# Per-token factors by a transpose and a DRAM round trip, and a two-pass chunk, in a three-branch trunk layer

## The chip, the cores and the metric

The kernel runs on one core of one Trainium2 chip, in one launch. The metric is the device time of that core in microseconds (us). TensorE is written PE, VectorE DVE, ScalarE ACT, GpSimd POOL and SyncE, which issues nearly all DMAs here, SP.

## What is computed

One decoder layer over 2048 tokens of width 1024, with 16 meta tokens in front. The reference, cut to what matters:

```python
xn = rms_norm(h, norm_w)
proj = jnp.einsum('btd,dn->btn', xn, w_in)          # 12*512 + 8 + 3*1024 columns
q = rms_norm(heads(sb_q), sb_qn); k = rms_norm(heads(sb_k), sb_kn)
o_sb = stick_breaking_attention(q, k, v, valid) * silu(sb_z)
beta = sigmoid(gd_b) * vmask                        # gd_b, gd_a: 4 columns each
g = -exp(a_log) * softplus(gd_a + dt_bias)
o_gd = rms_norm(gated_delta_rule_chunked(l2_norm(gq), l2_norm(gk), gv, beta, g)) * silu(gd_z)
o_hg = rms_norm(hgrn2_chunked(silu(hg_q), hk, hg_i * vmask, log(forget))) * silu(hg_z)
y = sum(sigmoid(mix[b]) * (o_b @ w_branch[b]) for b in (sb, gd, hg))
out = h + y @ w_out
```

All of it is float32. The norms of x, of the attention's keys and of the gated branch's keys each give one factor per token.

## The kernel before

Activations lie transposed: 128 features on the partitions, tokens along the free axis. The sequence is worked in four passes (`j` = 0 to 3) of 512 tokens; pass 0 also carries the 16 meta tokens, in columns 0 to 15 of tiles 528 wide. A float32 product is made of three matmul passes on rounded parts (`mm3`, L146: high times high, high times low, low times high), so one **chunk** (128 output columns of the projection, `proj`, L206) is 8 x 3 = 24 matmul passes of 512 columns, in pass 0 twice 24 of 264 columns where the meta tokens are needed. `load_w` (L126) brings a chunk's weights in two halves. In pass 0 it loads raw weights (two buffers `wraw`), has ACT round them (L136) and POOL or DVE subtract (L110), and writes both parts back to DRAM (L140); in later passes it reads them back (L132). Either way they go into five half-chunk buffers, `w2`.

The dense work is one Python generator, `dense_work` (L1219). For each pass it projects four attention heads (key, query, value, gate: `sb_proj`, L305), the chunk of the eight columns `gd_b` and `gd_a` (`gdn_rows`, L501), the gated heads (key, query, value: `gdn_proj`, L599), and then branch products with their gates, the third branch's projections, and the output product. Each chunk ends with `yield END`. The loop at L1292 weaves the sequential parts (the attention `sb_scan`, `gdn_mats`, `gdn_scan`, `hg_scan`) into it: `adv(n)` runs the dense work alone for n chunk ends, `weave(scan, us, n)` lets a scan run beside n of them. A pass has 85 ends.

Small steps behind a chunk are put off: `later(fn)` runs `fn` after the next chunk's matmuls, `later2` after the one behind that. The framework's scheduler then fixes one order of instructions for each engine; every engine and the SP queue work theirs in that order. There are three PSUM banks `acc` for the dense work, and 18 buffers `D` of 128 x 528 in SBUF for most of its tiles.

The steps that the change touches:

- **A factor per token, for all features.** `sum_cols` (L259) transposes squares to tokens on partitions (L276) and adds them up, one column per 128 tokens; `rsqrt` (L112) takes the power on POOL (L117). To multiply a tile with features on the partitions, the factor is needed as a row repeated on every partition. `row_bcast` (L152) makes it on PE: each column, broadcast to 128 columns, is transposed against the identity, four times for the four token blocks (L156) and once more, 16 columns wide, for the meta tokens (L160). The result stays in a PSUM bank `acc`.
- **Its readers.** The norm of x copies it to a `D` tile (L250), which `norm_x` (L178) multiplies with. `sb_proj` does it after the query's sums: one `rsqrt` for key and query, then in `post_r` (L341), behind the gate chunk, the transposes, the multiplication L343, a rounding on ACT (L344) and a subtraction. `gdn_proj` does the same in its `post_r` (L624) with the multiplication L626.
- **The chunk of eight columns.** `gdn_rows` runs `proj` over 128 columns of which eight (0 to 3, 32 to 35) are not zero, copies 36 rows out of PSUM (L506) and transposes them in four blocks (L515), 36 wide.

Of the kernel before, what the change touches and what calls it, by code (L numbers as in the profile page):

```python
# [7 lines left out]
F32 = mybir.dt.float32  # L8
# [7 lines left out]
P = 128  # L16
D = 1024
# [22 lines left out]
def kernel(  # L40
# [45 lines left out]
    def p_acc():  # L86
        return ps_acc.tile([P, 512], F32, tag="acc", name=nm("acc"))
# [63 lines left out]

    def row_bcast(r, cols, mcol):  # L152

        pt = p_acc()
        for n, c in enumerate(cols):
            nc.tensor.transpose(pt[:, n * P : (n + 1) * P], r[:, c : c + 1].broadcast_to([P, P]), ident)  # L156
        res = [(slice(META, WQ), pt)]
        if mcol is not None:
            pm = p_acc()
            nc.tensor.transpose(  # L160
                pm[:, :META], r[:META, mcol : mcol + 1].broadcast_to([META, P]), ident[:META, :META]
            )
            res.append((slice(0, META), pm[:, :META]))
        return res

# [6 lines left out]
    def norm_x(j, xt, rb):  # L172

        c0 = 0 if j == 0 else META
        xh, xl = [], []
        for k in range(KC):
            t = xt[k]
            nc.vector.scalar_tensor_tensor(  # L178
                t[:, c0:], t[:, c0:], nw[:, k : k + 1], rb[:, c0:], ALU.mult, ALU.mult
            )  # L180
# [42 lines left out]
    def norm_stats(j):  # L223
# [15 lines left out]
        ncol = NT + (j == 0)  # L239
        rb = slot("D")  # L240

# [6 lines left out]
        def bcast(r):  # L248
            for sl, v in row_bcast(r, list(range(NT)), NT if j == 0 else None):
                nc.scalar.copy(rb[:, sl], v)  # L250

# [53 lines left out]
    def sb_proj(j, xs, h, st):  # L305
# [10 lines left out]
        v_ = cols_tile(j)  # L316
        later(lambda: sum_cols(sq, v_, 0, 8 if m0 else None))
        yield END
# [14 lines left out]
        def post_q():  # L333
            sum_cols(sq2, v_, 4)
            ncol = 8 + m0
            r = rsqrt(v_[:, :ncol], P, ncol)
            nc.vector.tensor_copy(rq[:, :NT], r[:, NT : 2 * NT])
            nc.vector.tensor_scalar(rq[:, NT:], r[:, NT : 2 * NT], -1.0, None, ALU.mult)
            later(lambda: post_r(r))

        def post_r(r):  # L341
            for sl, v in row_bcast(r, list(range(NT)), 8 if m0 else None):
                nc.vector.scalar_tensor_tensor(kraw[:, sl], kraw[:, sl], wk, v, ALU.mult, ALU.mult)  # L343
# [157 lines left out]
    def gdn_rows(j, xs, st):  # L501
# [3 lines left out]
        raw = slot("D")  # L505
        yield from proj(j, xs, CH_BA, True, lambda ps, a, b: nc.scalar.copy(raw[:36, a:b], ps[:36]))  # L506
        nt = NT + m0
# [4 lines left out]
        def post():  # L512
            pt = p_acc()
            for n in range(NT):
                nc.tensor.transpose(  # L515
                    pt[:, n * 36 : n * 36 + 36], raw[:36, META + n * P : META + (n + 1) * P], ident[:36, :36]
                )
            c8 = slot("c8", (P, 2, H, 5), F32, 1)
            if m0:
                nc.gpsimd.memset(c8, 0.0)  # L520
                pm = p_acc()
                nc.tensor.transpose(pm[:META, :36], raw[:36, :META], ident[:36, :36])
                for q in range(2):
                    nc.vector.tensor_copy(c8[:META, q, :, 4], pm[:META, 32 * q : 32 * q + H])
            ptv = pt[:, : NT * 36].rearrange("p (n c) -> p c n", n=NT)
            for q in range(2):
                nc.vector.tensor_copy(c8[:, q, :, :NT], ptv[:, 32 * q : 32 * q + H])
            nc.scalar.activation(bcol[:, :, :nt], c8[:, 0, :, :nt], AF.Sigmoid)
# [70 lines left out]
    def gdn_proj(j, xs, hs, st):  # L599
# [5 lines left out]
        def head(h):  # L605
# [11 lines left out]
            def post_q():  # L617
                sum_cols(sqq, v_, 4)
                ncol = 8 + m0
                r = rsqrt(v_[:, :ncol], P, ncol)  # L620
                nc.vector.tensor_scalar(aq, r[:, 4:8], SCALE, None, ALU.mult)
                later(lambda: post_r(r))

            def post_r(r):  # L624
                for sl, v in row_bcast(r, list(range(NT)), 8 if m0 else None):
                    nc.vector.tensor_mul(kk[:, sl], kk[:, sl], v)  # L626

# [664 lines left out]
    for j in range(nq):  # L1292
        adv(5)
        sb_us = 4 * (2.0 + 2.7 * j) + 0.8 * (5 + 4 * j)
# [98 lines left out]
```

## Time and profile before

| | |
|---|---|
| median of 3 runs | 2872.62 us (2872.39 to 2875.82) |
| the profiled execution: its time | 2878.11 us |
| the profiled execution: its span | 2876.0 us |
| PE busy | 2786.5 us, 97% |
| DVE, ACT, POOL busy | 1524.5, 932.1, 760.0 us |
| DMA | 522.74 MB, 182 GB/s on average |
| granted PE clock | 0.993 |

All shares are of the span. A row of the groups gives line, engine, operation, tiles (out<-in), shape and count, then the busy time in all and the mean duration in ns of one, and behind a second bar the engine's idle time just before, with what ended it. Matmuls overlap: a row of the timeline gives the start, so the distance of two starts is what one of them adds. A row of the waits reads: engine and line that waited, engine and line waited for, us in total, times, longest. For DMAs the last number is the time from issue to landing.

### The profile page before, as it was taken

The numbers are of one execution on the slowest core, as the hardware profiler recorded it, in microseconds if no ns is written. First come the engines' busy times: TensorE is split into PE (matmuls) and PEld (weight loads), VectorE is DVE, ScalarE is ACT, GpSimd is POOL, SyncE is SP. The second block draws the span as 40 slices with busy tenths as digits, with TensorE's granted clock in tenths as the row PEclk, the third lists the DMA queues.
The fourth block names the chain that finished last, engine by engine and source line by source line (L and its number), as shares of the span: only waits on it lengthen the run. The fifth ranks groups of instructions, "written<-read, shape, count | busy, mean of one in ns | idle before, by whom it ended". The sixth has DMA issues, their size and how long they took to land.

```text
span 2876.0 us, 42134 instructions
## 1 busy us (share of the span) xinstructions
PE 2786.5 (97%) x15691; PEld 2325.4 (81%) x15691; DVE 1524.5 (53%) x3069; ACT 932.1 (32%) x2123; POOL 760.0 (26%) x1012
## 2 busy tenths in 40 slices
PE   5999999998999999999999999999999999999999
PEld 4898788886788888888888888888888777787887
DVE  4467637635257543654156855555415677627521
ACT  4555233333245312113045531211314555121110
POOL 4556213333123401212022421111302233302111
PEclk9999999999999999999999999999999999999999
DMA  6667655667754664446754456344674443653546
GB/s 203 237 214 230 230 193 189 227 233 260 252 170 148 193 181 133 139 153 226 227 190 163 155 161 186 106 142 147 227 227 147 141 139 125 197 155 103 155 153 212
DMA packets 198288, 522.74 MB, mean 182 GB/s; under 512 B 40448, under 2 KB 41536, under 8 KB 198084
## 3 DMA queue, kind: packets, MB, share of 16 engines
q1 hardware_dynamic: 197796, 519.98, 55.6%
q8 instruction: 124, 2.03, 0.3%
q14 instruction: 80, 0.66, 0.1%
q10 hardware_dynamic: 288, 0.07, 0.0%
HBM read 399.13 MB, written 120.84 MB: 181 GB/s over the span
## 4 chain that ended last, share of the span: by engine, by line
PE 81%; DVE 7%; DMA 6%; ACT 2%; POOL 2%; issue 1%; SPq 1%; ACTq 0%; DVEq 0%; POOLq 0%
PE acc L147 21%; PE acc L149 21%; PE acc L148 20%; DMA wraw<-in_w_in_dram 2%; PE z L1011 2%; PE tr L445 2%; PE acc L276 1%; PE av L147 1%; PE av L148 1%; PE av L149 1%; PE z L147 1%; PE z L149 1%; PE z L148 1%; DVE D L178 1%; DMA wraw<-in_w_out_dram 1%
## 5 line engine op out<-in xcount | busy, mean ns | idle before, releaser
L147 PE MATMUL acc<-xh,w 128*128 128x512 f32 (+1 forms) x2568 | 989.8, 386 | 15.4 <-ACT w L136 4.1
L149 PE MATMUL acc<-xh,w 128*128 128x512 f32 (+1 forms) x2568 | 974.6, 380 | 0.4 <-POOL w L110 0.4
L148 PE MATMUL acc<-xl,w 128*128 128x512 f32 (+1 forms) x2568 | 966.6, 376 | 7.9 <-DVE xl L110 7.9
L147 PEld LDWEIGHTS acc<-xh,w 128*128 128x128 f32 x2568 | 486.9, 190 | 97.0 <-ACT w L136 4.2
L148 PEld LDWEIGHTS acc<-xl,w 128*128 128x128 f32 x2568 | 487.5, 190 | 88.1 <-DVE xl L110 8.4
L149 PEld LDWEIGHTS acc<-xh,w 128*128 128x128 f32 x2568 | 485.6, 189 | 85.6 <-POOL w L110 0.8
L110 POOL TENSOR_TENSOR w<-wraw,w 128x512 fp32r<-128x512 f32 x110 | 145.4, 1323 | 346.7 <-ACT w L136 327.9
L136 ACT CAST w<-wraw 128x512 fp32r<-128x512 f32 x186 | 115.0, 618 | 251.9 <-DMA wraw<-in_w_in_dram 104.8
L421 POOL TENSOR_TENSOR S<-S,S 128x256 f32<-128x256 f32 (+2 forms) x108 | 95.2, 882 | 382.9 <-DVE S L413 217.5
L413 DVE TENSOR_TENSOR_SCAN S<-S,cc,zero 128x272 f32<-128x272 f32 (+2 forms) x152 | 144.1, 948 | 82.2 <-ACT S L407 81.7
L147 PE MATMUL acc<-ob,w 128*128 128x512 f32 x384 | 156.4, 409 | 11.9 <-DVE D L1083 5.5
L407 ACT ACTIVATE S<-z,rq 128x128 f32<-128x128 f32 (+4 forms) x216 | 116.8, 541 | 129.1 <-PE z L149 95.2
L148 PE MATMUL acc<-ob,w 128*128 128x512 f32 x384 | 153.4, 400 | 0.0
L149 PE MATMUL acc<-ob,w 128*128 128x512 f32 x384 | 152.3, 397 | 0.0
L592 DVE SCALAR_TENSOR_TENSOR D<-D,cw,D 128x512 f32<-128x512 f32 (+1 forms) x144 | 125.2, 869 | 23.1 <-ACT D L590 20.7
L110 DVE TENSOR_TENSOR S<-tr,S 128x512 fp32r<-128x512 f32 (+4 forms) x176 | 105.1, 606 | 39.8 <-ACT S L449 39.1
L1085 POOL TENSOR_TENSOR y<-y,g 128x512 f32<-128x512 f32 x32 | 49.7, 1558 | 285.8 <-DVE g L1083 285.8
L1067 ACT ACTIVATE g<-acc 128x512 f32<-128x512 f32 x64 | 38.3, 598 | 261.9 <-PE acc L149 247.2
L116 POOL TENSOR_SCALAR nu<-nv 128x8 f32<-128x8 f32 (+4 forms) x40 | 15.3, 383 | 397.2 <-DVE nv L888 231.1
L408 ACT ACTIVATE S<-z,rq 128x128 f32<-128x128 f32 (+4 forms) x216 | 116.3, 538 | 0.0
L449 ACT CAST S<-tr 128x512 fp32r<-128x512 f32 (+4 forms) x176 | 91.0, 529 | 59.4 <-PE tr L445 58.1
L445 PE MATMUL tr<-ident,S 128*128 128x128 f32 (+1 forms) x608 | 100.9, 273 | 3.9 <-POOL S L421 3.2
(325 smaller groups left out, 4700.7 us busy)
## 6 DMA issues: line engine op xcount, KB each, us to landing
w<-wk SPq DMA_DIRECT2D x558, 512.0 KB, 3.5
wk<-w SPq DMA_DIRECT2D x186, 512.0 KB, 2.9
wraw<-in_w_in_dram SPq DMA_DIRECT2D x146, 256.0 KB, 3.8
D<-in_xq_dram SPq DMA_DIRECT2D x56, 256.0 KB, 4.7
S<-rows SPq DMA_DIRECT2D x48, 256.0 KB, 4.5
S<-dv SPq DMA_DIRECT2D x48, 256.0 KB, 4.5
out_dram<-D SPq DMA_DIRECT2D x32, 256.0 KB, 4.7
S<-dk SPq DMA_DIRECT2D x24, 264.0 KB, 4.0
```

The source lines that it names most:

```text
L110: (eng or nc.gpsimd).tensor_sub(out_, a, hi.bitcast(F32))
L136: nc.scalar.copy(hi, raw)
L147: nc.tensor.matmul(dst, lh, rh, start=first, stop=False)
L148: nc.tensor.matmul(dst, lh, rl, start=False, stop=False)
L149: nc.tensor.matmul(dst, ll, rh, start=False, stop=last)
L407: nc.scalar.activation(pc[:, :n], z[:, :n], AF.Sigmoid, scale=rq[:, NT + i : NT + i + 1])
L408: nc.scalar.activation(at[:, :n], z[:, :n], AF.Sigmoid, scale=rq[:, i : i + 1])
L413: nc.vector.tensor_tensor_scan(pc[:, 0:n][:, ::-1], pc[:, 0:n][:, ::-1], zero1.broadcast_to([P, n]), 1.0 if carry[i] is None else carry[i] ...
L421: eng.tensor_mul(at[:, :n], at[:, :n], pc[:, 1 : n + 1])
L445: nc.tensor.transpose(tr[:kw, i * P : (i + 1) * P], ats[i][:, a - lo : a - lo + kw], ident)
L449: nc.scalar.copy(ath[:kw, cs_], tr[:kw, cs_])
L592: nc.vector.scalar_tensor_tensor(dst[:, c0:], raw[:, c0 + i : c0 + i + n], cw[:, ci, i : i + 1], dst[:, c0:], ALU.mult, ALU.add)
```

## The change

There are three edits.

1. `factor_rows` takes the place of `row_bcast`, except in the norm of pass 0. It transposes the factors as they are, up to 9 columns at once (L156 of the new code), copies the result to a small tile on ACT, writes its rows to a line in DRAM (L160; L162 for the meta tokens) and reads that line back, broadcast to 128 partitions, into a `D` tile (L165). Both DMAs are on SP's queue; the read waits for the write.
2. The key's power is taken by itself, right behind the key's sums, and the query's by itself. The factor of a key is transposed after the value chunk's query step (`post_q`) and used after the chunk behind it (`post_r`). In `gdn_proj` one more step (`post_rows`) stands between, so the multiplication is a chunk later. `adv(5)` at the start of a pass becomes `adv(6)`, and the `adv(17)` at its end `adv(16)`.
3. The chunk of eight columns packs the high and the low parts of its weights side by side into one 128-column weight (columns 0 to 63 and 64 to 127) and runs it over the high and the low parts of x: 16 passes. One half-chunk buffer holds it. The two parts of the result are added after the transposes, which are 100 wide now.

```diff
-    def row_bcast(r, cols, mcol):
+    def factor_rows(r, cols, mcol):
+        ncol = max(cols[-1], mcol or 0) + 1
         pt = p_acc()
-        for n, c in enumerate(cols):
-            nc.tensor.transpose(pt[:, n * P : (n + 1) * P], r[:, c : c + 1].broadcast_to([P, P]), ident)
-        res = [(slice(META, WQ), pt)]
+        nc.tensor.transpose(pt[:ncol, :P], r[:, :ncol], ident)
+        row = slot("junk", (P, P), F32, 2)
+        nc.scalar.copy(row[:ncol], pt[:ncol, :P])
+        d_ = dram.tile([WQ], F32, name=nm("fr"))
+        nc.sync.dma_start(d_[META:].rearrange("(n t) -> n t", t=P), row[cols[0] : cols[-1] + 1])
         if mcol is not None:
...
-        return res
+            nc.sync.dma_start(d_[:META].rearrange("(n t) -> n t", n=1), row[mcol : mcol + 1, :META])
+        c0 = META if mcol is None else 0
+        rb = slot("D")
+        nc.sync.dma_start(rb[:, c0:], d_[c0:].rearrange("(n t) -> n t", n=1).broadcast_to([P, WQ - c0]))
+        return rb
...
-        later(lambda: sum_cols(sq, v_, 0, 8 if m0 else None))
+        r_ = []
+        def post_k():
+            sum_cols(sq, v_, 0, NT if m0 else None)
+            r_.append(rsqrt(v_[:, : NT + m0], P, NT + m0))
+        later(post_k)
...
         def post_q():
-            sum_cols(sq2, v_, 4)
...
+            vq = cols_tile(1)
+            sum_cols(sq2, vq, 0)
+            r = rsqrt(vq[:, :NT], P, NT)
...
-            later(lambda: post_r(r))
+            rb = factor_rows(r_[0], list(range(NT)), NT if m0 else None)
+            later(lambda: post_r(rb))
-        def post_r(r):
-            for sl, v in row_bcast(r, list(range(NT)), 8 if m0 else None):
-                nc.vector.scalar_tensor_tensor(kraw[:, sl], kraw[:, sl], wk, v, ALU.mult, ALU.mult)
+        def post_r(rb):
+            nc.vector.scalar_tensor_tensor(kraw[:, c0:], kraw[:, c0:], wk, rb[:, c0:], ALU.mult, ALU.mult)
...
-        yield from proj(j, xs, CH_BA, True, lambda ps, a, b: nc.scalar.copy(raw[:36, a:b], ps[:36]))
...
+            for k in range(KC):
+                for i in range(2):
+                    nc.tensor.matmul(
+                        ps, pk[:, k], xs[i][k][:, a:b], start=k == 0 and i == 0, stop=k == KC - 1 and i == 1
+                    )
...
+            nc.scalar.copy(raw[:100, a:b], ps[:100])
...
-            def post_r(r):
-                for sl, v in row_bcast(r, list(range(NT)), 8 if m0 else None):
-                    nc.vector.tensor_mul(kk[:, sl], kk[:, sl], v)
+            def post_rows(r):
+                rb = factor_rows(r, list(range(NT)), 8 if m0 else None)
+                later(lambda: post_r(rb))
+            def post_r(rb):
+                nc.vector.tensor_mul(kk[:, c0:], kk[:, c0:], rb[:, c0:])
...
-        adv(5)
+        adv(6)
...
-        adv(17)
+        adv(16)
```

Where this moves instructions is shown at one place, the first attention head of pass 1; numbers behind a tile's name only tell tiles apart. On PE before: `acc_7899` is the head's gate chunk, `nr_7886` the factors, `D_7849` the values, `acc_7955` the next head's key chunk.

```order
L147 MATMUL acc_7899<-xh_7423,w_1634_7897 128x512
L148 MATMUL acc_7899<-xl_7424,w_1634_7897 128x512
L149 MATMUL acc_7899<-xh_7423,w_1634_7897 128x512
L156 MATMUL acc_7926<-ident,nr_7886 128x128 x4
L276 MATMUL acc_7938<-ident,D_7849 128x128 x4
L147 MATMUL acc_7955<-xh_7388,w_1644_7951 128x512
```

On PE now: `acc_7872` is the value chunk, `D_7821` the query's squares, `nr_7860` the key's factors, `acc_7926` the gate chunk.

```order
L148 MATMUL acc_7872<-xl_7438,w_1655_7870 128x512
L149 MATMUL acc_7872<-xh_7437,w_1655_7870 128x512
L287 MATMUL acc_7899<-ident,D_7821 128x128 x4
L156 MATMUL acc_7911<-ident,nr_7860 4x128
L147 MATMUL acc_7926<-xh_7402,w_1668_7922 128x512
```

The factor's transpose moved from behind the gate chunk to ahead of it. On DVE before, at the same head: L343 multiplies the key, `D_7771`, by its factor in `acc_7926`, and L285 evacuates the gate chunk.

```order
L263 TENSOR_REDUCE nv_7804<-acc_7880 128x4
L337 COPY rq_7846<-nr_7886 128x4
L338 TENSOR_SCALAR rq_7846<-nr_7886 128x4
L343 SCALAR_TENSOR_TENSOR D_7771<-D_7771,wk,acc_7926 128x512
L285 TENSOR_TENSOR D_7894<-acc_7899,D_7894 128x512
L110 TENSOR_TENSOR D_7893<-acc_7938,D_7892 128x512
```

On DVE now: L360 is the key's multiplication, its factor `D_7917` the tile that the DMA fills, and L296 the gate's evacuation.

```order
L274 TENSOR_REDUCE nv_7898<-acc_7899 128x4
L354 COPY rq_7864<-nr_7905 128x4
L355 TENSOR_SCALAR rq_7864<-nr_7905 128x4
L360 SCALAR_TENSOR_TENSOR D_7785<-D_7785,wk,D_7917 128x512
L296 TENSOR_TENSOR D_7921<-acc_7926,D_7921 128x512
L110 TENSOR_TENSOR D_7920<-acc_7960,D_7919 128x512
```

The multiplication kept its place among DVE's instructions, and reads a tile from a DMA instead of a PSUM bank. On SP's queue before, at the same head (`w_1656` and `w_1657` are the two halves of the next head's query chunk):

```order
L132 DMA w_1634_7897<-wk_477 128x1024
L132 DMA w_1644_7951<-wk_553 128x1024
L132 DMA w_1645_7953<-wk_560 128x1024
L132 DMA w_1656_8001<-wk_641 128x1024
L132 DMA w_1657_8003<-wk_648 128x1024
```

On SP's queue now: the two DMAs stand among the loads of weights for the gate chunk's successors (`w_1685` and `w_1686` are the two halves of the next head's query chunk).

```order
L132 DMA w_1679_7975<-wk_566 128x1024
L132 DMA w_1685_8008<-wk_632 128x1024
L160 DMA fr_7915<-junk_7913 4x128
L165 DMA D_7917<-fr_7915 128x512
L132 DMA w_1686_8010<-wk_639 128x1024
L132 DMA w_1700_8069<-wk_706 128x1024
```

The write and the read are new, and every load behind them waits until the read has been issued.

More of the change, by code (lines that the diff above doesn't have):

```diff
@@ L239, in norm_stats @@
         ncol = NT + (j == 0)
-        rb = slot("D")
+        rb = [None]
         def sums():
@@ L248, in bcast @@
         def bcast(r):
-            for sl, v in row_bcast(r, list(range(NT)), NT if j == 0 else None):
-                nc.scalar.copy(rb[:, sl], v)
+            if j:
+                rb[0] = factor_rows(r, list(range(NT)), None)
+                return
+            rb[0] = slot("D")
+            pt = p_acc()
+            for n in range(NT):
+                nc.tensor.transpose(pt[:, n * P : (n + 1) * P], r[:, n : n + 1].broadcast_to([P, P]), ident)
+            nc.scalar.copy(rb[0][:, META:], pt)
+            pm = p_acc()
+            nc.tensor.transpose(pm[:, :META], r[:META, NT : NT + 1].broadcast_to([META, P]), ident[:META, :META])
+            nc.scalar.copy(rb[0][:, :META], pm[:, :META])
         if j == 0:
@@ L515, in post @@
                 nc.tensor.transpose(
-                    pt[:, n * 36 : n * 36 + 36], raw[:36, META + n * P : META + (n + 1) * P], ident[:36, :36]
+                    pt[:, n * 100 : n * 100 + 100], raw[:100, META + n * P : META + (n + 1) * P],
+                    ident[:100, :100],
                 )
```

49 lines of the change are left out of this document (34 added, 15 removed).

## The prediction

> **What bounds the kernel now.** I read the page's busy times first, then its chain of work, then PE's waits, the busy times by pass, and last the two shapes of matmul that the change touches.
>
> ```profile
> PE 2786.5 (97%) x15691; PEld 2325.4 (81%) x15691; DVE 1524.5 (53%) x3069; ACT 932.1 (32%) x2123; POOL 760.0 (26%) x1012
> PE 81%; DVE 7%; DMA 6%; ACT 2%; POOL 2%; issue 1%; SPq 1%; ACTq 0%; DVEq 0%; POOLq 0%
> ```
>
> PE is busy 97% of 2876.0 us, and 81% of the chain that ended last is its own work. The four passes over the sequence, from 36 us on (rows: stretch, its length, PE busy, PEld, DVE, ACT, POOL, granted clock, DMA share, GB/s):
>
> ```profile
> 36.00:720.00 684.00, 652.85 (x4156) 565.75 (x4154) 382.25 (x756) 272.46 (x627) 268.44 (x285) 0.99 0.66 223
> 720.00:1440.00 720.00, 717.08 (x3880) 593.10 (x3881) 349.02 (x727) 199.75 (x464) 151.75 (x222) 1.00 0.57 182
> 1440.00:2160.00 720.00, 712.83 (x3865) 589.07 (x3864) 381.54 (x773) 220.41 (x501) 162.38 (x244) 0.99 0.53 170
> 2160.00:2876.00 716.00, 696.65 (x3772) 572.13 (x3770) 389.37 (x778) 221.96 (x504) 162.20 (x234) 0.99 0.48 153
> ```
>
> PE stands for 31 us of the first pass and for 3, 7 and 19 us of the others. Hence matmul time taken out should come out of the span nearly whole, unless the new DMA trips make PE wait. What a matmul costs is not its mean duration: they overlap. Starts on PE (start, busy, line):
>
> ```profile
> 865.78 0.60 PE L156 MATMUL acc<-ident,nr 128*128 128x128 f32 x4
> 866.22 0.60 PE L276 MATMUL acc<-ident,D 128*128 128x128 f32 x4
> 866.66 0.38 PE L445 MATMUL tr<-ident,S 128*128 128x128 f32 x2
> 999.67 0.39 PE L147 MATMUL acc<-xh,w 128*128 128x512 f32 x1
> 999.90 0.39 PE L148 MATMUL acc<-xl,w 128*128 128x512 f32 x1
> 1000.13 0.39 PE L149 MATMUL acc<-xh,w 128*128 128x512 f32 x1
> 164.02 0.28 PE L148 MATMUL acc<-xl,w 128*128 128x264 f32 x1
> 164.14 0.29 PE L149 MATMUL acc<-xh,w 128*128 128x264 f32 x1
> ```
>
> Four transposes take 0.44 us from start to next start, 0.11 each; a pass of 512 columns 0.23; one of 264 columns 0.12. A chunk of 24 passes takes 24 x 0.23 = 5.5 us.
>
> **PE work removed.** The rows of the broadcast transposes by shape:
>
> ```profile
> L156 PE MATMUL acc<-ident,nr 128*128 128x128 f32 x144 | 22.6, 277 | 4.1 <-POOL nr L117 4.1
> L160 PE MATMUL acc<-ident,nr 16*128 16x16 f32 x9 | 2.1, 231 | 0.0
> L515 PE MATMUL acc<-ident,D 36*128 36x36 f32 x16 | 1.7, 232 | 0.0
> ```
>
> L156 ran 144 = 36 x 4 times. The first group (the norm of pass 0) stays; 35 groups go from four to one: 35 x 3 x 0.11 = 11.6 us. Eight of the nine 16-column ones go too, at most 0.23 each and at least nothing; I take 0.1, as a short member of a burst: 0.8 us. The chunk of eight columns drops 8 of 24 passes: three passes over the sequence x 8 x 0.23 = 5.5, and 2 x 8 x 0.12 = 1.9 in pass 0, together 7.4 us. Added: the 17 transposes behind that chunk stream 100 columns, not 36; between nothing and 17 x 0.11 = 1.9, and since 128 columns cost 0.11 while 36 cost not much less in a burst, I take 0.3. Sum on PE: 11.6 + 0.8 + 7.4 - 0.3 = 19.5 us.
>
> The trap is the mean of 277 ns: by it the 105 transposes would be 29 us. The Trainium skill (TensorE: Matmul & The Clock Gate, Part 4) gives about 275 ns for a PE transpose in a kernel's context; by that figure the sum on PE would be 37 us. The row of four in 0.44 us decides for 0.11: 275 is how long one lasts, not what it adds.
>
> **What is added beside PE.** Each trip is: one transpose, an ACT copy out of PSUM (nearest are the two shapes of L250; ACT is 32% busy), a small write and a broadcast read on SP's queue. The nearest DMAs are the gates' rows, written in 8 KB and read back broadcast to 128 partitions in 256 KB:
>
> ```profile
> L250 ACT COPY D<-acc 128x512 f32<-128x512 f32 x4 | 2.3, 581 | 0.0
> L250 ACT COPY D<-acc 128x16 f32<-128x16 f32 x1 | 0.2, 176 | 0.0
> S<-rows SPq DMA_DIRECT2D x48, 256.0 KB, 4.5
> rows<-D SPq DMA_DIRECT2D x12, 8.0 KB, 2.1
> L671 SPq DMA_DIRECT2D S<-rows x48: 319/422/1464, 204.4 to 2481.3; - x48
> DMA to landing us min/median/max: 3.7/4.5/6.6
> ```
>
> A trip is therefore 0.2 (the copy: 128 columns, between the two rows) + 0.4 + 2.1 + 0.4 + 4.5 = 7.6 us behind its transpose; 6.8 with the fastest read, 9.7 with the slowest. What covers it is one chunk, as the two pieces of order shown with the change say: on PE the factor's transpose moved from behind the head's gate chunk (acc_7899 before, acc_7926 now) to ahead of it, and on DVE the multiplication of k by its factor (L343 before, L360 now) did not move. It still stands ahead of the gate's evacuation, L296, and now waits for a DMA. (For the gated keys, L679, both moved a chunk on; the distance is the same.) The trip of 7.6 us has 5.5 us of chunk to hide in, so DVE is held about 2 us, and behind it in its queue L296, which frees the gate's PSUM bank. PE needs that bank only a chunk later (three banks, and the next chunk runs in another), 5.5 us: the hold is covered in dense stretches. Where a scan is woven in, DVE's next products are wanted sooner. The trips of this kind are 16 for k and 16 for the gated keys: 32 x 2 = 64 us of holds. How much of a hold reaches PE I take from the holds that exist: DVE waits for the very transposes, and PE waits for these DVE lines to free banks.
>
> ```profile
> L343 DVE SCALAR_TENSOR_TENSOR D<-D,wk,acc 128x512 f32<-128x512 f32 x16 | 11.8, 738 | 13.0 <-PE acc L156 13.0
> L626 DVE TENSOR_TENSOR D<-D,acc 128x512 f32<-128x512 f32 x16 | 10.8, 676 | 11.6 <-PE acc L156 11.6
> PE acc L147 <- DVE D L343: 1.2, 3, 0.4
> PE acc L276 <- DVE D L343: 0.7, 1, 0.7
> PE acc L276 <- DVE D L626: 0.7, 1, 0.7
> PE acc L641 <- DVE D L626: 0.2, 1, 0.2
> ```
>
> 24.6 us of holds cost PE 2.8 us, 11%. So 64 us cost about 7.0, and the old 2.8 go: +4.2 us net. Bounds: 2.8 gained (no hold arrives) and 61 lost (every hold does).
>
> The Trainium skill (DMA: Bandwidth & Descriptors, Anatomy of one DMA) puts a DMA at about 2.0 us fixed, mostly the receipt of the write, plus its bytes at 436 GB/s, and so speaks against a DRAM trip in place of on-chip work. By its figures the two would be an estimated 2.0 + 2.6 us, inside one chunk, and the sum would be 19.5 + 2.8 gained; the median of 4.5 us for the read says 2 us of hold instead.
>
> On SP a trip's read waits for its write, so the weight loads behind it stand 2.1 + 0.4 + 0.4 = 2.9 us. From pass 1 on that is free: SP itself waits for PE to free weight buffers,
>
> ```profile
> SPq L132 <- PE acc L149: 1532.1, 495, 16.1
> w<-wk SPq DMA_DIRECT2D x558, 512.0 KB, 3.5
> ```
>
> five half-chunk buffers give a lead of four halves, 11 us, against 2.9 + 3.5. In pass 0 the raw weights go through two buffers and each half is written back on the same queue, so there the cover is thin: 8 trips x 2.9 = 23 us of queue time. PE now waits for the splits there only this long (36 to 720 us):
>
> ```profile
> PE acc L147 <- ACT w L136: 4.2, 2, 4.1
> PE acc L149 <- DVE w L110: 0.8, 1, 0.8
> PE acc L149 <- POOL w L110: 0.8, 2, 0.4
> ```
>
> 5.8 us in all, so I count nothing for it and keep it as a rival. The rest is small. The three trips for the norms have four products of 12 passes, 11 us, ahead of their first reader. POOL takes the keys' and queries' powers apart, four columns each where it took eight:
>
> ```profile
> L117 POOL TENSOR_TENSOR nr<-nu,mhalf 128x8 f32<-128x8 f32 x24 | 44.3, 1845 | 1.8
> L117 POOL TENSOR_TENSOR nr<-nu,mhalf 128x4 f32<-128x4 f32 x19 | 19.7, 1037 | 1.6
> ```
>
> that is 16 x 0.23 us more and 16 more additions, the keys' a chunk ahead of need, on an engine 26% busy. The 32 added tiles take turns in the 18 D buffers, so a read may have to wait for a buffer; no row shows that, and the bounds of the holds stand for it. Scans begin one chunk end later with as much dense work under them. The last one of a pass so ends a chunk nearer to the product that reads its head:
>
> ```profile
> 1313.96 0.60 PE L276 MATMUL tr<-ident,S 128*128 128x128 f32 x4
> L110 POOL TENSOR_TENSOR ob<-S,ob x2: 1293/1296/1298, 1316.0 to 1322.0; 128x512 fp32r<-128x512 f32 x2
> ```
>
> From the transposes at 1313.96 to the split's end at 1316.0 + 1.3 are 3.4 us, and PE's order now has 24 passes, 5.5 us, between the two (35 before): I count nothing; with that cover gone it would be at most 3.4 us a pass.
>
> **Sum.** 19.5 - 4.2 = 15.3 us less. The profiled execution took 2878.11 us, 2.1 around its span, and lies 5.5 above the median of 2872.62: 2862.8 for it, 2857.3 for the median. I say 2857.
>
> **Rivals.**
> - *DVE's holds reach PE (slower).* Place: the scans of passes 1 to 3, where DVE's scan, product and split feed PE's next transposes. For it: pass 3 already leaves PE 19 us idle, and the slowest read adds 2 us a trip. Against it: the 11%. It decides from 30% on (19.5 of 64). At half, 32 - 2.8 - 19.5 = +10: 2882. Chance 0.09.
> - *Pass 0's weight feed pays.* 23 us of SP time; half of it on the path: 2857 + 11 = 2868, no change that can be told. For it: 66% DMA share and 31 us idle in pass 0. Against: 5.8 us of waits for splits. Chance 0.13.
> - *The trips hide whole.* The read lands within the chunk: 2872.6 - 19.5 - 2.8 = 2850. Chance 0.10. The medians above make it the lesser case. The Trainium skill's figures for a DMA, above, would make the trip one of this kind.
> - *Transposes cost their whole duration*, 0.277 each: 18 us more gained, 2840. Chance 0.02: the starts speak against it. The Trainium skill's 275 ns, read as a cost, would give this.
> - That the change doesn't do what it says I exclude: PE's order shows one transpose in place of four and 16 passes in that chunk.
>
> **Numbers.** My forecast of 2857 has 0.66. A measurement tells about 0.2%, 5.7 us, from no change. Faster: 0.66 + 0.10 + 0.02 = 0.78; same: the feed, 0.13; slower: 0.09. The range runs from 2846 (all hidden, and the short transposes at their upper bound and a few waits gone) to 2871 (the feed's half and some of the holds), leaving out the slower case and the transposes.
>
> **What would show it.** Right: some 105 transposes fewer in the group of 128-column ones on ident and nr, PE's busy time down by about 19 us, DVE waiting for the factor's DMA 1 to 3 us some 30 times, PE's waits up by under 8. Wrong: landing times of the read above 7 us; PE waiting for the split weights in pass 0 by over 15 us; PE's waits for DVE or ACT lines in the scans up by over 20; or PE's busy time down by nearly 40.

## The result and the profile after

The changed kernel is slower: 2915.93 us (median of 4 runs, 2910.88 to 2918.51) against 2872.72 us, ratio 1.014 with a 95% interval of 1.0124 to 1.0155. The profiled execution took 2913.99 us. The sum had promised 15 us less; it is some 43 more, so 58 us are to be found.

Busy times and chain of the page after:

```profile
PE 2787.0 (96%) x15538; PEld 2321.4 (80%) x15538; DVE 1518.2 (52%) x3073; ACT 935.9 (32%) x2155; POOL 774.2 (27%) x1042
PE 77%; DMA 9%; DVE 7%; POOL 3%; ACT 2%; issue 1%; SPq 1%; ACTq 0%; POOLq 0%; DVEq 0%
```

The edit is all there: 153 matmuls fewer, which is 35 x 3 + 8 + 40. Yet PE's busy time is the same (2786.5 before). PE had to run more of its work at a lower clock: the mean granted clock fell from 0.993 to 0.986, and 1.4% of 2912 us is 41 us, where 0.7% of 2876 was 20. So the clock ate what the missing matmuls saved, and nearly all that the span grew by is time in which PE stood: 125.2 us (2912.2 less 2787.0), where it was 89.5. By pass, in the columns of the table before:

```profile
36.00:720.00 684.00, 633.38 (x3999) 550.66 (x3998) 375.67 (x744) 267.98 (x628) 269.61 (x289) 0.97 0.64 215
720.00:1440.00 720.00, 710.39 (x3805) 585.19 (x3805) 347.03 (x726) 198.95 (x465) 149.22 (x230) 1.00 0.58 186
1440.00:2160.00 720.00, 707.70 (x3815) 582.74 (x3814) 377.26 (x766) 218.51 (x503) 164.31 (x246) 0.99 0.54 173
2160.00:2912.00 752.00, 727.58 (x3898) 596.61 (x3896) 395.92 (x800) 233.11 (x530) 176.06 (x253) 0.99 0.49 156
```

In pass 0 PE now stands for 51 us of 684 (31 before) at 0.97 (0.99). PE's waits of the whole run that grew:

```profile
PE acc L147 <- DVE D L1136: 16.0, 3, 7.5
PE acc L156 <- POOL nr L117: 11.2, 4, 5.7
PE acc L147 <- DVE D L296: 6.5, 3, 2.5
PE acc L544 <- DVE D L296: 2.9, 1, 2.9
```

L1136 is the evacuation of a branch product, which stands behind the norm's multiplications (L1083 before, 5.5 us in all). L296 evacuates the gate chunk and stands behind a key's multiplication (L285 before, 1.0 us). POOL's power cost PE 0.8 us at the keys before: of the 4.1 us of its old row, 3.3 belong to the norm of pass 0, which has a line of its own now. All of L296's 9.4 us and 10.9 of the power's 11.2 lie between 36 and 345 us, in the heads of pass 0. And DVE waits for the factors 30 times, as foretold, but 92.5 us in all:

```profile
L180 DVE SCALAR_TENSOR_TENSOR D<-D,nw,D 128x512 f32<-128x512 f32 (+1 forms) x32 | 30.5, 1022 | 14.9 <-DMA D<-fr 10.4 <-ACT D L261 4.5
L360 DVE SCALAR_TENSOR_TENSOR D<-D,wk,D 128x512 f32<-128x512 f32 (+1 forms) x16 | 14.0, 875 | 42.6 <-DMA D<-fr 42.5
L679 DVE TENSOR_TENSOR D<-D,D 128x512 f32<-128x512 f32 (+1 forms) x16 | 12.7, 792 | 39.6 <-DMA D<-fr 39.6
```

How one such hold reaches PE is seen in pass 0, at a gated head. DVE's timeline (start, duration, line, and in brackets the idle time before it with its cause):

```profile
218.05 0.76 DVE L642 SCALAR_TENSOR_TENSOR D<-D,cw,D 128x528 f32<-128x528 f32 x1
222.00 1.38 DVE L679 TENSOR_TENSOR D<-D,D 128x528 f32<-128x528 f32 x1 [3.20 <-DMA D<-fr]
223.31 0.75 DVE L642 SCALAR_TENSOR_TENSOR D<-D,cw,D 128x528 f32<-128x528 f32 x1
```

ACT's, in which L642's reader stands ahead of the rounding of the next weights (L136):

```profile
220.85 0.74 ACT L640 ACTIVATE D<-D,cw 128x528 f32<-128x528 f32 x1
226.00 0.65 ACT L645 ACTIVATE D<-D 128x528 f32<-128x528 f32 x1 [4.41 <-DVE D L642]
226.55 0.36 ACT L637 COPY D<-acc 128x264 f32<-128x264 f32 x1
228.69 0.63 ACT L664 ACTIVATE D<-D 128x512 f32<-128x512 f32 x1 [1.78 <-DVE D L646]
229.22 0.61 ACT L136 CAST w<-wraw 128x512 fp32r<-128x512 f32 x1
```

POOL's, where the split (L110) waits for that rounding and the power (L117) stands behind it and all that follows it:

```profile
229.91 1.38 POOL L110 TENSOR_TENSOR w<-wraw,w 128x512 fp32r<-128x512 f32 x1 [7.08 <-ACT w L136]
...
240.78 1.82 POOL L117 TENSOR_TENSOR nr<-nu,mhalf 128x9 f32<-128x9 f32 x1
```

And PE's, where the next head's factor transpose waits for that power:

```profile
236.52 0.28 PE L148 MATMUL acc<-xl,w 128*128 128x264 f32 x1
236.64 0.28 PE L149 MATMUL acc<-xh,w 128*128 128x264 f32 x1
242.66 0.38 PE L156 MATMUL acc<-ident,nr 128*9 128x128 f32 x1 [5.73 <-POOL nr L117]
...
244.34 0.42 PE L149 MATMUL acc<-xh,w 128*128 128x264 f32 x1
244.56 0.42 PE L147 MATMUL acc<-xh,w 128*128 128x264 f32 x1
```

DVE's 3.20 us are followed by 4.41 on ACT, 7.08 on POOL and 5.73 on PE. Not all of this is new: at the same head of the kernel before, DVE stood 0.67 and 1.50 us, ACT 2.82, POOL 5.33, and PE 2.02 (for an ACT copy, not for the power). What came on top is 1.0, 1.6, 1.8 and 3.7 us. Behind it passes of 264 columns start 0.22 us apart, where they had 0.12. The Trainium skill (TensorE: Matmul & The Clock Gate, Part 1) says that the array runs at half clock after a window of some 3.4 us in which it was idle; here the clock granted from 242 to 249 us was 0.53. This chain is one place read closely. Whether holds like it cause the loss is what the runs below have to show.

### The profile page after: what moved, and what is told of

It reads as the page before. It is cut to its first block, busy times and chain, and to the rows that moved or that the text cites. A ratio compares the mean times of both kernels' runs of the same rounds, so it can differ in the third digit from the quotient of the medians.

```text
span 2912.2 us, 41970 instructions
## 1 busy us (share of the span) xinstructions
PE 2787.0 (96%) x15538; PEld 2321.4 (80%) x15538; DVE 1518.2 (52%) x3073; ACT 935.9 (32%) x2155; POOL 774.2 (27%) x1042
## 3 DMA queue, kind: packets, MB, share of 16 engines
q8 instruction: 123, 2.02, 0.3%
## 4 chain that ended last, share of the span: by engine, by line
PE 77%; DMA 9%; DVE 7%; POOL 3%; ACT 2%; issue 1%; SPq 1%; ACTq 0%; POOLq 0%; DVEq 0%
PE acc L147 20%; PE acc L149 19%; PE acc L148 19%; DMA wraw<-in_w_in_dram 3%; PE z L1064 2%; PE tr L462 2%; POOL w L110 1%; DVE S L430 1%; PE acc L287 1%; PE av L147 1%; PE av L148 1%; DMA D<-fr 1%; PE av L149 1%; DMA wraw<-in_w_out_dram 1%; DVE D L180 1%
## 5 line engine op out<-in xcount | busy, mean ns | idle before, releaser
L147 PE MATMUL acc<-xh,w 128*128 128x512 f32 (+1 forms) x2528 | 978.9, 387 | 16.3 <-DVE D L296 6.5
L149 PE MATMUL acc<-xh,w 128*128 128x512 f32 (+1 forms) x2528 | 961.9, 381 | 1.5 <-POOL w L110 1.5
L148 PE MATMUL acc<-xl,w 128*128 128x512 f32 (+1 forms) x2528 | 952.6, 377 | 7.9 <-DVE xl L110 7.9
L110 POOL TENSOR_TENSOR w<-wraw,w 128x512 fp32r<-128x512 f32 (+1 forms) x108 | 151.8, 1406 | 332.4 <-ACT w L136 284.3
L136 ACT CAST w<-wraw 128x512 fp32r<-128x512 f32 x184 | 113.5, 619 | 277.2 <-DMA wraw<-in_w_in_dram 129.9
L147 PE MATMUL acc<-ob,w 128*128 128x512 f32 x384 | 156.5, 411 | 13.5 <-DVE D L1136 8.5
L116 POOL TENSOR_SCALAR nu<-nv 128x4 f32<-128x4 f32 (+4 forms) x56 | 21.1, 376 | 461.1 <-DVE nv L941 239.1
L110 DVE TENSOR_TENSOR S<-tr,S 128x512 fp32r<-128x512 f32 (+4 forms) x176 | 104.9, 605 | 68.4 <-ACT S L466 68.2
L642 DVE SCALAR_TENSOR_TENSOR D<-D,cw,D 128x512 f32<-128x512 f32 (+1 forms) x144 | 121.5, 845 | 20.7 <-ACT D L640 18.9
L110 DVE TENSOR_TENSOR w<-wraw,w 128x512 fp32r<-128x512 f32 x78 | 57.4, 737 | 121.0 <-ACT w L136 120.2
L274 DVE TENSOR_REDUCE nv<-acc 128x4 f32<-128x512 f32 x68 | 46.4, 683 | 131.1 <-PE acc L287 120.1
```

What stands on the lines that cost most here:

```text
L110: (eng or nc.gpsimd).tensor_sub(out_, a, hi.bitcast(F32))
L136: nc.scalar.copy(hi, raw)
L147: nc.tensor.matmul(dst, lh, rh, start=first, stop=False)
L148: nc.tensor.matmul(dst, lh, rl, start=False, stop=False)
L149: nc.tensor.matmul(dst, ll, rh, start=False, stop=last)
L642: nc.vector.scalar_tensor_tensor(dst[:, c0:], raw[:, c0 + i : c0 + i + n], cw[:, ci, i : i + 1], dst[:, c0:], ALU.mult, ALU.add)
```

## The experiments

All ratios are to the kernel before on the same chip; 0.1% is 2.9 us. Four sets of runs: the parts alone, the waits taken out, the weights' feed, and what stayed open.

### The parts alone

**x1_chunk**: the kernel before with the chunk of two passes (the edit of `gdn_rows`) and nothing else.

> The kernel before with the two-pass chunk alone (no trips, schedule as before). If the trips' holds are the cause of the loss, the chunk is innocent and gives what its 24 + 16 removed passes are worth, 7 us: about 2865. If the chunk itself costs (wider transposes, one weight buffer for two halves, its own generator), it is slower than before, 2880 or more. If the shifted schedule is the cause, 2865 as well.

Measured 1.0018 (1.0004 to 1.0031). **Missed**: 7.4 us less of matmuls gave nothing. Matching ACT's evacuations one by one in the two traces, they gain about 2 us in each of passes 1 and 2, but in pass 0 a lead of 8.8 us at 326 us has become 2.2 us of delay at 576. PE's waits from 330 to 740 us, where the first row was 4.2 us before and the second 0.3 (there L949):

```profile
PE acc L147 <- ACT w L136: 11.5, 4, 6.1
PE acc L982 <- ACT kmt L980: 5.2, 2, 2.8
PE acc L149 <- DVE w L110: 2.3, 2, 1.3
```

Of the 11 us lost, 7.3 are new waits for rounded weights. That the weights' feed takes the lead is a guess here; x13_beforeraw3, below, comes back to it.

**x2_shift**: the schedule's ends alone.

```diff
-        adv(5)      # start of a pass
+        adv(6)
-        adv(17)     # its end
+        adv(16)
```

> The kernel before with the schedule's shift alone: 6 instead of 5 chunk ends ahead of the scans, 16 instead of 17 behind them. If the trips' holds are the cause, this is within 4 us of 2872.7. If the shift is the cause, because every scan ends one chunk nearer to its reader, this takes most of the loss: 2895 to 2915.

Measured 1.0053 (1.0038 to 1.0068), 15 us, with not one instruction added: between the two theories. The edit that I had counted at nothing costs as much as the whole gain that I had forecast.

**x14_chunkshift**: both of these, and still no trips.

> The kernel before with the chunk of two passes and the schedule's ends at 6 and 16, and no trips at all: what the change would be without its main part. If the parts add up, 0.18% + 0.53% over the kernel before, ratio 1.005 to 1.009, and the 35 trips then cost another 0.5 to 0.9% beyond the 11 us of transposes that they save. If the shift's cost is one that the chunk's shorter work takes away, or that only shows beside the trips' waits, ratio under 1.003.

Measured 1.0066 (1.0051 to 1.0081): the two add up. What the trips do is the step from here to 1.014.

**x3_trips**: the change without the chunk's edit.

> The changed kernel with the chunk of eight columns as it was, 24 passes: trips and shift alone. If the trips' holds are the cause, it loses the chunk's 7 us again: about 2923. If the chunk were the cause, it would be near 2870.

Measured 1.0143 (1.0118 to 1.0168), as the whole change. Seven us more than the change's 1.0140 lie inside this interval too, so this run doesn't tell what the chunk is worth there.

**x4_norm**: the change with the three norms' factors made on chip again.

```diff
-            if j:
-                rb[0] = factor_rows(r, list(range(NT)), None)
-                return
```

> The changed kernel with the three norms' factors made by four transposes and an ACT copy again; the keys' trips stay. If DVE's hold at the norm's eight multiplications is part of the loss (PE waited 7.5, 4.5 and 4.1 us for the third branch's products there, 3.2, 1.2 and 1.2 before), 8 to 16 us come back with the clock's share: 2900 to 2908. If the shift of the schedule is what makes those products late, nothing comes back: 2913 to 2918.

Measured 1.0111 (1.0096 to 1.0126): three trips cost some 8 us by the medians of the ratios, though the intervals overlap a little. PE's wait for that product falls from 16.0 to 4.8 us. One norm in the changed kernel, on DVE:

```profile
1377.00 0.69 DVE L1140 TENSOR_TENSOR D<-y,D 128x512 f32<-128x512 f32 x1
1381.88 6.40 DVE L180 SCALAR_TENSOR_TENSOR D<-D,nw,D 128x512 f32<-128x512 f32 x8 [4.19 <-DMA D<-fr]
1388.21 0.67 DVE L1136 TENSOR_TENSOR D<-D,acc 128x512 f32<-128x512 f32 x1
```

### The waits taken out

**x6_noread**: the read takes a row of the weights, so that it waits for no write.

```diff
-        nc.sync.dma_start(rb[:, c0:], d_[c0:].rearrange("(n t) -> n t", n=1).broadcast_to([P, WQ - c0]))
+        nc.sync.dma_start(rb[:, c0:], w_in[0][0:1, c0:WQ].broadcast_to([P, WQ - c0]))
```

> The changed kernel, but the broadcast read of a factor (L165) takes a row of the inputs' weights, and not the row just written: the write is still issued, the read has nothing to wait for. The keys and the normalised sequence so get a wrong factor; transposes, copies, DMA bytes, shift and chunk stay. Theory 1 (the trips' waits pay: DVE's products of a norm or of a key standing in its queue for the read, and SP standing 2.1 us for the write): all that the trips added goes, and what is left is the shift's 15 us less some of the work saved on PE, about 2885 us where the kernel before takes 2876 (ratio 1.001 to 1.006). Theory 2 (the trips pay by what isn't a wait for the DMA: POOL's powers split in two, the added DMA bytes in pass 0, the buffers): near the changed kernel, 2910 or more (ratio over 1.011).

Measured 1.0082 (1.0062 to 1.0103), between the two. It took away less than I had meant: the read still stands in SP's queue behind weight loads that wait for buffers, and DVE still waits for it 43.4 us in all. It also changed an order: with no write to wait for, some reads were put ahead of the writes (at the end of pass 1, L165 at 1354.75 us and L160 at 1355.27). **Inconclusive** by itself.

**x5b_const**: nobody waits for the read; the multiplications take constants, and the true factors are left out.

```diff
-            nc.vector.scalar_tensor_tensor(kraw[:, c0:], kraw[:, c0:], wk, rb[:, c0:], ALU.mult, ALU.mult)
+            nc.vector.scalar_tensor_tensor(kraw[:, c0:], kraw[:, c0:], wk, fixf[:, 1:2].broadcast_to([P, WQ - c0]), ALU.mult, ALU.mult)
```

(and so for L180 and L679)

> The changed kernel, in which DVE multiplies the keys and the normalised sequence of passes 1 to 3 by constant columns (1.0, 0.26, 0.08) in place of the rows read back, so the true factors are left out there: the transposes, the copies, the writes, the reads and SP's wait for each write all stay, and only nobody waits for the read to land. Theory 1 (DVE standing 82 us at the keys and 10 at the norms is what the trips cost): what is left is the shift and the chunk, near the kernel with both and no trips less the work saved on PE, 2870 to 2885 (ratio 0.998 to 1.003). Theory 2 (half of the cost is SP's stand at each write and POOL's split powers): 2893 to 2903 (ratio 1.006 to 1.010).

Measured 1.0068 (1.0053 to 1.0083). Without the holds the change is faster by 1.0140 less 1.0068, 0.72% or 21 us. But this run takes away more than the holds: the scheduler puts a multiplication that waits for no factor earlier in DVE's order. At the first key of pass 2 it stands right behind the key's evacuation,

```profile
1425.55 0.75 DVE L363 SCALAR_TENSOR_TENSOR D<-D,wk,fixf 128x512 f32<-128x512 f32 x1 [5.50 <-ACT D L326]
```

and in the changed kernel, which is 19 us behind x5b_const by then, behind the query's factors:

```profile
1462.22 0.75 DVE L360 SCALAR_TENSOR_TENSOR D<-D,wk,D 128x512 f32<-128x512 f32 x1 [4.24 <-DMA D<-fr]
```

So the 21 us are what the holds and the multiplications' place cost together; no run parts the two in every pass. The figure is theory 2's, its reason isn't: what is left equals x14_chunkshift, which has neither trips nor SP's stand. From 36 to 345 us, of x14_chunkshift,

```profile
36.00:345.00 309.00, 298.02 (x1929) 265.68 (x1929) 175.70 (x338) 143.53 (x318) 149.20 (x180) 0.99 0.68 230
```

of x5b_const,

```profile
36.00:345.00 309.00, 292.19 (x1881) 259.85 (x1881) 172.57 (x330) 139.64 (x324) 152.60 (x195) 0.99 0.70 234
```

and of the changed kernel.

```profile
36.00:345.00 309.00, 279.54 (x1814) 251.74 (x1813) 151.58 (x278) 136.94 (x316) 154.64 (x189) 0.97 0.66 220
```

With the holds PE stands for 13 us more than without (309 - 279.54 against 309 - 292.19), and runs at a clock 0.02 lower, another 6: 19 of the 21 us lie in the first eighth of the run. The same evacuations on ACT, matched one by one, come so many us later than in the kernel before (first column: their time there; then x14_chunkshift, x5b_const, x4_norm and the change):

```
us     chunkshift  const   norm on chip  changed
  41      -1.4     -1.1       -1.3         -1.0
 326      -4.1      0.9       17.6         17.9
1316       7.9      8.1       24.2         24.4
1418       9.3     12.0       25.6         30.8
2026       9.7      7.8       23.8         27.6
2129      11.4     11.2       25.8         32.9
2783      14.0     15.5       31.1         35.0
```

By 326 us the trips cost 22.0 us (17.9 and 4.1), 17.0 of it gone with the holds. One evacuation is good to some 2 us: at the next three, 331 to 349 us, the two figures are 20.2 to 22.1 and 18.0 to 19.5. Behind that the change loses 17.1 more, the kernel without trips 18.1: there the trips gain 1.0 us. With the norms on chip the loss is 13.5, so the key trips of passes 1 to 3 gain 4.6 of the 24 x 3 x 0.11 = 7.9 us that they save, holds and all. The norms give the rest back at the ends of passes 1 and 2 (1316 to 1418 and 2026 to 2129 us: 6.4 and 5.3 us in the change, 1.4 and 2.0 with the norms on chip). With constants 3.9 and 3.4 are lost there, so the norms' loss isn't the holds alone.

**x7_pass0**: pass 0's eight key factors on chip, the other trips kept.

> The changed kernel with pass 0's eight key factors (four attention, four gated heads) spread on chip by four transposes again; trips through DRAM from pass 1 on, shift and chunk as changed. Theory 1 (the key trips cost in pass 0, where the weights' feed has no slack and SP, POOL and DVE stand in it): the delay of 25 us at the end of pass 0 falls to about 5, and the time to 2892 to 2900 (ratio about 1.007). Theory 2 (they cost evenly, by DVE's holds in every pass): a quarter of some 20 us goes, 2911 or so (ratio about 1.012).

Measured 1.0087 (1.0067 to 1.0106), at the upper edge of theory 1. Eight of 35 trips carry 15 us of the loss. DVE's holds of those eight, in the changed kernel from 36 to 345 us:

```profile
DVE D L360 <- DMA D<-fr: 14.3, 4, 4.9
DVE D L679 <- DMA D<-fr: 8.6, 4, 3.2
```

23 us of holds cost 15 to 19 there. Here the attention keys' multiplications stand ahead of the gate's evacuation, as in the change, and not where x5b_const has them; but the added copies, writes and reads of the eight trips go with the holds. The other 70 us cost little: from 326 to 2783 us the change loses 17.1 us and x5b_const 14.6. One reason is seen behind the two multiplications shown above. Where the change holds DVE for 4.24 us, x5b_const has nothing to wait for but the gate chunk, and DVE stands as long:

```profile
1443.56 0.69 DVE L299 TENSOR_TENSOR D<-acc,D 128x512 f32<-128x512 f32 x1 [4.37 <-ACT D L297]
```

**x9_nogated**: trips for norms and attention keys only, which need no shift.

> The changed kernel without the gated keys' trips (four transposes on chip, one chunk earlier, as before) and with the old ends of the schedule, 5 and 17, which these trips alone had forced; the trips of the norms and the attention keys and the chunk stay. Theory 1 (the shift costs 15 us and the trips of the gated keys about half of what the key trips cost, 10): about 2890 (ratio 1.003 to 1.007). Theory 2 (the trips of norms and attention keys cost nearly all): 2905 or more (ratio over 1.009). Theory 3 (all but the norms' 7 us lies with the gated keys): 2880 (ratio 1.000 to 1.002).

Measured 1.0059 (1.0042 to 1.0076), theory 1. Without the shift, and without the gated keys' trips that forced it, the change is still slower.

### The weights' feed

**x10_raw3**: x1_chunk with a third raw buffer.

```diff
-        "D": 18, "S": 21, "g": 2, "y": 8, "ob": 8,
+        "D": 18, "S": 20, "g": 2, "y": 8, "ob": 8,
-                raw = wpool.tile([P, 512], F32, tag="wraw", name=nm("wraw"), bufs=2)
+                raw = wpool.tile([P, 512], F32, tag="wraw", name=nm("wraw"), bufs=3)
```

> The kernel before with the chunk of two passes alone (as in the run of the chunk alone), and a third buffer for the raw weights, for which the scans give up one of 21 buffers of their kind. Theory 1 (the chunk's gain in pass 0 is given back to the weights' feed, which waits for one of two raw buffers): with a third buffer the gain stays, 8 to 15 us less than the chunk alone (ratio 0.993 to 0.998 against the kernel before). Theory 2 (the feed is bound by the DMA bytes or by the rounding on ACT, not by the buffers): as the chunk alone, ratio 1.000 to 1.003. If the buffer taken from the scans is missed, slower than that, with PE waiting for scans' products in passes 1 to 3.

Measured 0.9924 (0.9909 to 0.9938), 2852.77 us: the fastest of all, ahead of both kernels, and 27 us below x1_chunk, where theory 1 had 8 to 15. Of the waits of the same stretch, 330 to 740 us, those for rounded weights are all but gone (largest row and L136's):

```profile
PE acc L147 <- DVE D L1116: 3.4, 1, 3.4
...
PE acc L147 <- ACT w L136: 0.8, 1, 0.8
```

**x13_beforeraw3**: the third buffer alone.

> The kernel before with the third raw buffer and 20 for the scans, and nothing else, to tell the chunk's own worth from the buffer's. Theory 1 (the chunk of two passes saves the predicted 7.4 us of matmuls where the feed doesn't take it back): 6 to 10 us slower than the third buffer with the chunk, ratio 0.9945 to 0.9965. Theory 2 (the chunk saves nothing that counts): as with it, ratio 0.992 to 0.993.

Measured 0.9930 (0.9916 to 0.9945), theory 2: the gain is the buffer's, and theory 1 of x10_raw3 is refuted. With the feed relieved the chunk's 7.4 us come to 2.7 in the matched instructions, which the ratios can't tell from none. By pass, they say where the 7.4 went. In passes 1 to 3 the chunk gains 4.4 us of the 5.5 foretold (4.6 without the third buffer). In pass 0, where 1.9 were foretold, x10_raw3 leads x13_beforeraw3 by 3.8 us at 326 us and is 1.7 behind at 744; without the buffer it is 3.7 behind. So the feed isn't all that takes the lead in pass 0; what else does stays open.

**x12_afterraw3**: the third buffer in the changed kernel.

> The changed kernel with the third buffer for raw weights and 20 buffers for the scans, as in the run that did this to the chunk alone, where it was worth 0.94%. Theory 1 (the trips' cost in pass 0 is that of a weights' feed without slack): the third buffer takes back the 28 us that it took there and most of the 15 that the eight key trips of pass 0 cost, ratio 0.998 to 1.002 against the kernel before. Theory 2 (the trips' cost has nothing to do with the feed): the same 28 us and no more, ratio 1.003 to 1.006. Theory 3 (with the trips in the way the feed no longer sets the pace in pass 0): less than 15 us gained, ratio over 1.009.

Measured 1.0101 (1.0084 to 1.0118), theory 3: 11 us gained, where the buffer took 20 off the kernel before. With the trips in the way the feed isn't what sets the pace in pass 0: from 36 to 720 us PE waits 8.0 us for POOL's power (three times) and not once for L136.

### What stayed open

**x15_shiftgdnhg** and **x16_shifthg** split the shift: gated and last heads' scans one end later, and the last heads' alone.

```diff
         for h in range(H):
             obs[0, h] = weave(sb_scan(j, h, sst), sb_us, 4 + (h == H - 1))
+        adv(1)                                  # x15; x16: adv(6) ahead of hg_scan 0 and 1
...
-        adv(17)
+        adv(16)
```

> The kernel before, in which only the gated and the last heads' scans begin one chunk end later (one chunk end between the attention scans and the gated matrices, 16 at the pass's end), and the attention scans stay: no trips, no chunk edit. Theory 1 (the shift costs where the attention scans stand, whose work grows from pass to pass): ratio 0.999 to 1.002. Theory 2 (it costs in the gated or the last heads' scans): ratio 1.004 to 1.007, as the whole shift. Theory 3 (every scan that meets other chunks pays its part): 1.002 to 1.004.

> The kernel before, in which only the last heads' scans (the third kind) begin one chunk end later: no trips, no chunk edit. If the last heads' scans carry the shift's cost: ratio 1.004 to 1.007. If they carry none: 0.999 to 1.001. If each kind pays its part: 1.001 to 1.003.

Measured 1.0038 (1.0023 to 1.0053) and 1.0017 (1.0007 to 1.0027): steps of 0.17% for the last heads', 0.21% for the gated and 0.15% for the attention scans (x2_shift less x15). Both runs came out where every kind pays its part, and no one kind carries the whole. The second step is barely clear of its intervals, the third not.

**x18_latetrips**: x10_raw3 with trips for the twelve attention keys of passes 1 to 3.

> The version with the chunk of two passes and the third raw buffer, with trips for the attention keys of passes 1 to 3 alone, where no weights are split and the schedule need not shift: 12 groups of four transposes go to one, 12 x 3 x 0.11 = 4.0 us. Theory 1 (outside of pass 0 DVE's holds of some 3 us reach PE in small part): 1 to 4 us less than without them, ratio 0.991 to 0.992. Theory 2 (they reach PE by a third or more there too, 12 us or more): 8 us or more slower than without them, ratio 0.995 and up.

Measured 0.9935 (0.9922 to 0.9948) against 0.9924: between the two theories, and not told apart from x10_raw3. DVE stood 30.5 us in twelve holds. Even in its best place a trip brings nothing that this could measure.

## Why the prediction was wrong

Forecast 2857, range to 2871, 0.78 for faster; it came out 2916, slower. By its own steps:

- **"Sum on PE: 19.5 us", "should come out of the span nearly whole."** The count was right (153 fewer), the step to the span failed. The chunk gave nothing or 2.7 us for 7.4: in passes 1 to 3 its gain came (4.4 to 4.6 of 5.5), in pass 0 it turned into 1.7 to 3.7 us of loss. Of the transposes' 12 us some 5 come out where keys are factored behind pass 0, and the norms and pass 0 take them back: x5b_const, with all but the holds, equals x14_chunkshift. In pass 0 the feed is one cause: PE's waits for L136 grow from 4.2 to 11.5 us with the chunk and are 0.8 with a third buffer. It isn't the only one, since the chunk loses its lead there with the buffer too. I had the row, 4.2 us of waits for L136, and read it as the whole of the feed's bound; but a row of waits says how far PE is ahead now, not how much sooner the weights could come (the buffer alone gave 20 us).
- **"Scans begin one chunk end later with as much dense work under them."** This failed by 15 us (x2_shift), a fourth of the miss. I compared the amount of work under a scan, not what it is. Shown is the size, and that more than one kind of scan pays; which chunk collides with which step isn't.
- **"The trip of 7.6 us has 5.5 us of chunk to hide in, so DVE is held about 2 us."** The trip was right, the cover wrong. Over the 32 keys the median from the transpose's start to its reader is 7.2 us (9.4 in pass 0's heads). But the multiplication stands ahead of the gate's evacuation, so DVE reaches it before the chunk is over: 4.7 us behind the transpose, in the median of the held ones, and it stands 3.0. The keys' holds came to 82.1 us where I had 64, the norms' to 10.4 where I had none.
- **"24.6 us of holds cost PE 2.8 us, 11%."** The share is no constant: two thirds to four fifths in pass 0's heads, a few per cent behind them (2.5 of 70). The mean of the old holds lay mostly in places where they don't hurt. In pass 0 both ends of the argument failed. **"PE needs that bank only a chunk later"**: PE waited 9.4 us for L296 there, 1.0 before. And I didn't look at ACT, which waits for DVE in the convolution and is also the one that rounds weights; behind it stands POOL with the power, for which PE waited 10.9 us, 0.8 before. In x5b_const, which also takes the powers apart, PE waits 2.7 us for that evacuation there and not once for a key's power.
- **"Pass 0's weight feed pays", chance 0.13.** The place was right, the carrier wrong. I had priced SP's stand, 23 us; x5b_const keeps SP's wait for the writes (41.9 us in all, 48.2 in the change), and of the 22.0 us in pass 0's heads 5.0 are left. Nor does PE wait for weights: from 36 to 720 us 1.7 us for L136, 4.2 before. The hold passes through the feed's engines, ACT and POOL, at the place read above, and reaches PE as the late power.
- **The slower rival, chance 0.09,** had the mechanism, holds that reach PE, and put it into passes 1 to 3. Shown are other places: pass 0's heads, and the norms at the pass ends.
- **"The three trips for the norms have four products of 12 passes, 11 us, ahead of their first reader."** DVE's order failed this: the eight L180 stand ahead of the next product's L1136, so a held norm holds the products at once: PE's wait for L1136 is 16.0 us, 4.8 with the norms on chip, and the ratios differ by 8 us (x4_norm).
- **"Up by under 8"** for PE's waits: the three pass ends alone are up by 10.5, all of them by 35.7. And half clock behind waits was no term of the sum.
- **"36 cost not much less in a burst"** was wrong and luckily cheap: in the burst of the kernel before they start 0.06 us apart (L515), the 100-wide ones now 0.09 (L560). By 17 x 0.024 = 0.4 us the term of 0.3 came out all the same.

The ledger: chunk and shift 0.66% (x14_chunkshift), holds and the multiplications' place 0.72% (x5b_const), together 1.38 of 1.40%. The trips' 12 us of saved transposes don't show in it: in x5b_const other costs of the trips take them back. Open stays what these are, some 2 to 5 us of them in pass 0's heads: of the added copies, writes, powers and buffer turns none was taken out alone.

## What to carry to other kernels

A hold on one engine is to be followed through every in-order queue that it blocks, to the one whose work feeds PE next; a mean share of holds that reach PE from elsewhere says nothing on a stretch where the engines hand work to and fro. A shift of a hand-made schedule is a cost to be measured alone before it is put to use for something else. Where a profile shows even a few us of waits for a feed, try one more buffer on it (0.70% here for one of 256 KB) before fewer matmuls. And a run that takes a wait away can also change the order of instructions, when a scheduler makes that order: compare the two orders before the difference is put down to the wait.

## What was not expected of the hardware

Half clock came without a long wait. At the end of pass 1 in x5b_const PE's waits were short: 1.01 and 1.33 us (and the start at 1344.63 is 0.80 long):

```profile
1342.11 0.50 PE L151 MATMUL acc<-ob,w 128*128 128x512 f32 x1 [1.01 <-POOL ob L113]
1344.63 0.80 PE L150 MATMUL acc<-xh,w 128*128 128x512 f32 x1 [1.33 <-ACT D L1123]
```

Busy times in stretches of 3.4 us around it (PE first, clock third from the end):

```profile
1337.70:1341.10 3.40, 3.40 (x15) 2.30 (x13) 3.40 (x7) 2.10 (x5) 0.70 (x1) 1.00 1.02 377
1341.10:1344.50 3.40, 1.20 (x5) 0.67 (x4) 3.40 (x5) 1.05 (x2) 0.95 (x1) 1.00 0.24 54
1344.50:1347.90 3.40, 3.27 (x8) 2.59 (x9) 3.40 (x7) 1.02 (x3) 0.24 (x1) 0.52 0.72 289
1347.90:1351.30 3.40, 3.40 (x16) 2.80 (x15) 1.91 (x2) 0.29 (x1) 3.09 (x2) 0.98 0.26 60
```

In one stretch PE was busy for 1.20 of 3.40 us, and the next ran at 0.52: two waits of 1.01 and 1.33 us cost about another 1.6, the half of the 3.4 that was not granted. The Trainium skill's rule (TensorE: Matmul & The Clock Gate, Part 1) speaks of a window that is idle; here one busy to a third was enough, and the measurement decides.
